# Hybrid attention and pooling layer on one Trainium2 core: key and weight buffers allocated in another order, and four re-orderings in the attention stage

## The chip, the cores and the metric

The kernel runs on 1 core of one Trainium2 chip. The core has a matrix engine (TensorE, PE in the profile, with its weight loads shown as PEld), a vector engine (VectorE, DVE), an activation engine (ScalarE, ACT), a general engine (GpSimd, POOL) and a queue engine that here only issues transfers (SyncE, SP). The metric is the device time of one execution in microseconds (us); the time before is 1195.26 us, the median of 3 runs (1193.7 to 1197.1).

## The reference

One layer on 4096 tokens of width 1024, in float32. The input is normalised and projected once; the projection splits into queries (8 heads of 64), keys and values (2 heads), an attention gate, a pooling input and a pooling gate. Attention is banded: a block of 128 queries sees the block before, its own and the one behind. The pooling half takes centred means over 2, 4, 8 and 16 tokens. Both halves are gated, projected back, normalised and added to the input:

```python
h = rmsnorm(x, pre_norm_g[l])
proj = jnp.einsum('bsd,de->bse', h, w_in[l])
q, k, v, g_a, u_p, g_p = jnp.split(proj, splits, axis=-1)
a = banded_attention(q, k, v, rel_bias, attn_sink[l]) * jax.nn.silu(g_a)
p = multiscale_pool(u_p, pool_w[l], pool_scale[l]) * jax.nn.silu(g_p)
mixed = jnp.einsum('bse,ed->bsd', jnp.concatenate([a, p], axis=-1), w_out[l])
x = x + rmsnorm(mixed, post_norm_g[l])
```

In banded_attention a softmax over up to 384 keys is taken with a relative bias and a sink logit per head.

## The kernel before

Every float32 operand is carried as a pair of float16 tensors (a high part and a rest), and a product is three float16 matmuls. A first stage (to about 500 us) normalises x, stores its pairs to a scratch in DRAM (x_scr) and makes the gates and the pooling half, which go to ga_scr and yp_scr. The last thing that it stores is the gate tile cc (transfers ga_scr<-cc, line L671).

The second stage handles the tokens backwards, in units of 256 tokens (unit 15 first) that hold two blocks of 128 (block 31 first). Its steps, with the names that the profile uses:

- proj_k, proj_v (matmuls kv, L1227 and L1373) and keep_k, keep_v: the projected keys and values lie in one PSUM accumulator. ACT writes a high part (L1216) and DVE the rest (L1217), keys into k_all, values into vv. A unit's keys and values leave in the order ACT keys, DVE keys, ACT values, DVE values.
- proj_q (aq, L1227), in two halves of four heads, and keep_q: ACT and DVE copy it to q.
- visit(b, half): scores (s, L1272) for four heads into two PSUM tiles s0 and s1, then softmax: logits (DVE, p<-s, L1295), exps (ACT, p<-p, L1306), denominators (DVE, L1313 and L1316), probs (ACT, the high part of pn, L1328), rests (DVE, the low part of pn, L1336) and turn (SP, a transposing transfer pt<-pn, L1345). Each of logits, exps, probs and rests is four instructions, one for each head.
- attend(b): values (o, L1417) reads pt and vv; gate (DVE, at, L1425); in an even block then sums (DVE, L1485, L1488, L1491). ACT and POOL split the results into pairs (y and ys, L1452 and L1456).
- the output projection of a unit, in seven products ("11", "22", "12", "s2", "s3", "s1", "s4") of twelve matmuls each (m and ms, L1550) against prepared weight tiles wo. Products go to PSUM accumulators acc0, acc1 and acc2. Product "12" adds onto "11" in acc0; then square (ACT, jkb<-m, L1573) and gain11 (DVE, mo<-m, L1578) both read acc0, the second of the two waiting for the first. The next matmuls into acc0 are the next unit's first half of aq.

The order of the second stage is written by hand. A list (plan) takes entries due(t, function); t is a planned time, not a measured one, and the whole list is sorted by t and emitted in that order. Each engine runs its own instructions strictly in that order. pe(us, ...) puts a TensorE step at the running time now[0] and moves it on. Most units follow one pattern; block 29 (b == NB - 3) is written out apart, because unit 15 is the first to be projected out. There do_kv(u - 1, 1) puts the keys and values of unit 13 into acc1, the accumulator that product "s2" of unit 15 writes next (mix_p6).

Buffers of the second stage come from a pool (pb1) that is laid over memory of the first stage. A tile's first write therefore waits for the first stage's last users of exactly that memory, and the order of allocation decides which users these are.

## Time and profile before

| | |
|---|---|
| median of 3 runs | 1195.26 us (1193.7 to 1197.1) |
| the profiled execution | 1197.77 us |
| its span | 1196.0 us |
| PE busy | 1158.1 us (97%) |
| DVE busy | 933.1 us (78%) |
| ACT busy | 701.2 us (59%) |
| POOL busy | 314.2 us (26%) |
| mean granted clock | 0.996 |

The span is what the trace covers; the time of the execution holds 1.77 us more. A busy time is the sum over an engine's instructions. The granted clock is the share of full speed that TensorE was given. In a row of the timeline the columns are start and duration in us, the engine, line, operation and tiles, how many instructions are merged (x), and in brackets the idle time ahead of it with what ended it. In a row of waits they are the waiting engine, tile and line, the releaser, and the total in us, the number of times and the longest. In a row of windows they are the stretch, its length, busy time of PE, PEld, DVE, ACT and POOL, the granted clock, the DMA share and GB/s.

### The profile page before, as it was taken

The numbers are of one execution on the slowest core, as the hardware profiler recorded it, in microseconds if no ns is written. First come the engines' busy times: TensorE is split into PE (matmuls) and PEld (weight loads), VectorE is DVE, ScalarE is ACT, GpSimd is POOL, SyncE is SP. The second block draws the span as 40 slices with busy tenths as digits, with TensorE's granted clock in tenths as the row PEclk, the third lists the DMA queues.
The fourth block names the chain that finished last, engine by engine and source line by source line (L and its number), as shares of the span: only waits on it lengthen the run. The fifth ranks groups of instructions, "written<-read, shape, count | busy, mean of one in ns | idle before, by whom it ended". The sixth has DMA issues, their size and how long they took to land. (4 is left out here: it accounts for less than half of the span.)

```text
span 1196.0 us, 31699 instructions
## 1 busy us (share of the span) xinstructions
PE 1158.1 (97%) x13176; PEld 890.0 (74%) x13176; DVE 933.1 (78%) x1834; ACT 701.2 (59%) x1459; POOL 314.2 (26%) x309
## 2 busy tenths in 40 slices
PE   5999999999999999898999999999999999999997
PEld 4998888888988888775667676676666767667643
DVE  6889996967888972567877877877787787787786
ACT  6865555645755531266575675666667567566662
POOL 0002111111101110202334433432533443354231
PEclk9999999999999999999999999999999999999999
DMA  9544587578657573487966875776886587587694
GB/s 322 202 124 150 168 287 233 180 232 270 211 176 250 158 205 103 149 219 188 243 174 135 204 191 114 199 197 152 180 203 159 138 203 192 124 189 162 160 236 124
DMA packets 292433, 224.51 MB, mean 188 GB/s; under 512 B 210704, under 2 KB 251920, under 8 KB 287680
## 3 DMA queue, kind: packets, MB, share of 16 engines
q1 hardware_dynamic: 292288, 222.48, 68.3%
q8 instruction: 103, 1.69, 0.6%
q14 instruction: 42, 0.34, 0.1%
HBM read 113.37 MB, written 60.33 MB: 145 GB/s over the span
## 5 line engine op out<-in xcount | busy, mean ns | idle before, releaser
L634 PEld LDWEIGHTS <-wq 128*128 128x128 f16 x4104 | 401.7, 98 | 52.7 <-issue 2.8
L634 PE MATMUL y<-xt,wq 128*128 128x256 f16 x1512 | 204.1, 273 | 0.9 <-ACT cc L742 0.9
L1306 ACT ACTIVATE p<-p,nm 128x385 f32<-128x385 f32 (+1 forms) x256 | 153.0, 599 | 59.6 <-POOL p L1289 38.0
L1227 PE MATMUL aq<-xb,xb 128*128 128x256 f16 x1024 | 174.9, 274 | 4.6 <-DVE mo L1578 4.6
L1336 DVE SCALAR_TENSOR_TENSOR pn<-p,rd,pn 128x384 f16<-128x384 f32 (+1 forms) x256 | 155.6, 654 | 26.1 <-ACT pn L1328 26.1
L1550 PE MATMUL ms<-wo,ys 128*128 128x512 f16 x720 | 162.7, 379 | 1.8 <-ACT pn L1328 1.8
L1295 DVE CUSTOM_DVE_ANT_0 p<-s,nt,nsink 128x384 f32<-128x384 f32 (+1 forms) x256 | 156.0, 666 | 1.5 <-PE s L1272 1.3
L1328 ACT ACTIVATE pn<-p,rd 128x384 f16<-128x384 f32 (+1 forms) x256 | 136.3, 596 | 23.6 <-ACT p L1306 21.7
L1227 PEld LDWEIGHTS <-xb 128*128 128x128 f16 x1280 | 125.8, 98 | 23.6 <-issue 6.7
L1227 PE MATMUL aq<-xb,xt 128*128 128x256 f16 x512 | 140.4, 274 | 0.0
L1550 PEld LDWEIGHTS <-ys 128*128 128x128 f16 x720 | 69.1, 98 | 83.6 <-issue 3.0
L304 POOL TENSOR_TENSOR yt<-yt,sg 128x512 f32<-128x512 f32 (+2 forms) x32 | 48.0, 1500 | 311.4 <-DVE yt L307 283.0
L1550 PE MATMUL m<-wo,y 128*128 128x512 f16 x540 | 119.6, 379 | 1.4 <-POOL y L1456 0.7
L1550 PEld LDWEIGHTS <-y 128*128 128x128 f16 x540 | 51.5, 98 | 64.8 <-issue 3.6
L1584 POOL TENSOR_TENSOR mo<-mo,gpost 128x512 f32<-128x512 f32 x39 | 63.6, 1630 | 85.6 <-ACT jkb L1573 84.5
L1313 DVE TENSOR_SCALAR den<-den 128x4 f32<-128x4 f32 x64 | 17.3, 271 | 76.9 <-ACT p L1306 76.8
L1417 PE MATMUL o<-pt,vv 128*64 128x256 f16 x1128 | 69.0, 274 | 3.9 <-DMA pt<-pn 3.4
L1227 PEld LDWEIGHTS <-xt 128*128 128x128 f16 x640 | 62.9, 98 | 12.9 <-issue 4.3
L634 PE MATMUL plain<-xb,wq 128*128 128x256 f16 x576 | 68.9, 277 | 3.0 <-ACT xb L446 1.8
L634 PE MATMUL y<-xb,wq 128*128 128x256 f16 x504 | 68.8, 273 | 0.0
L634 PE MATMUL v<-xb,wq 128*128 128x256 f16 x504 | 68.6, 273 | 0.2 <-DVE cc L304 0.2
L634 PE MATMUL v<-xt,wq 128*128 128x256 f16 x504 | 68.6, 273 | 0.0
(207 smaller groups left out, 1912.9 us busy)
## 6 DMA issues: line engine op xcount, KB each, us to landing
nt<-in_xT SPq DMA_DIRECT2D x28, 512.0 KB, 5.4
x_scr<-xb SPq DMA_DIRECT2D x14, 1024.0 KB, 7.2
xb<-x_scr SPq DMA_DIRECT2D x14, 1024.0 KB, 7.5
xr<-in_x SPq DMA_DIRECT2D x28, 512.0 KB, 4.4
out<-xr SPq DMA_DIRECT2D x28, 512.0 KB, 3.7
xn<-in_x SPq DMA_DIRECT2D x27, 512.0 KB, 4.5
ga_scr<-cc SPq DMA_DIRECT2D x64, 128.0 KB, 2.1
raw<-in_w_out SPq DMA_DIRECT2D x16, 512.0 KB, 5.3
```

The costliest lines, as they stand in the source:

```text
L304: eng.tensor_tensor(out=out, in0=in0, in1=in1, op=op)
L634: nc.tensor.matmul(b[:, s], wq[:, slot[q, op], wv, s, k, :], x[:, xv, k, :], start=(first and k + s + wv + xv == 0), stop=(last and k == H ...
L1227: nc.tensor.matmul(acc, w[:, j, k, :], x[:, kh, v, kt, :], start=(n == 0), stop=(n == 3 * KT - 1),)
L1295: nc.vector.tensor_tensor_reduce(out=p_t[b, half][:, hh, :nk], in0=s_t[jj][:, gg, :nk], in1=bias[:, h, lo : lo + nk], scale=negc[:, h : h ...
L1306: nc.scalar.activation(p[:, hh, : nk + 1], p[:, hh, : nk + 1], AF.Exp, bias=nm_t[b, half][:, hh : hh + 1], scale=-1.0, accum_out=den_t[b, ...
L1313: nc.vector.tensor_scalar(out=den, in0=den, scalar1=1.0 / P_SCALE, scalar2=None, op0=ALU.mult)
L1328: nc.scalar.activation(prob_view(b, half)[:, 0, i], p_t[b, half][:, i, :nk], AF.Copy, scale=rd_t[b, half][:, i : i + 1],)
L1336: nc.vector.scalar_tensor_tensor(out=pn4[:, 1, i], in0=p_t[b, half][:, i, :nk], scalar=rd_t[b, half][:, i : i + 1], in1=pn4[:, 0, i], op0= ...
L1417: nc.tensor.matmul(o_ps[a, 2 * half : 2 * half + 2], v[:, vi, kt, a], pt[b, half][:, pi, g, :, i, :], start=(n == 0), stop=(n == last),)
L1550: nc.tensor.matmul(z_t[u, tag], y[:, k, yi, :], wo[o][:, wi, k, :], start=(n == 0 and acc is None), stop=(n == 3 * HK - 1), skip_group_che ...
L1584: eng.tensor_tensor(out=mo, in0=mo, in1=gpost[:, cs], op=ALU.mult)
```

## The change

Four edits. First, k_all and gpost are allocated ahead of the weight tiles, and these in another order. Second, the second half of unit 15's queries is projected straight after the first half, and unit 14's keys and values come between the two visits of block 31. Third, in block 29 the visit's second half and then product "12" come ahead of attend(30), which comes ahead of unit 13's keys and values; before, attend(30) came first, then the visit, the keys and values, and product "12". Fourth, gain11 is due 1.2 before the product's end rather than 0.1 behind it, in every unit from 15 to 2.

```diff
--- before.py
+++ after.py
@@ -1193,15 +1193,15 @@
     ps_o = ctx.enter_context(tc.tile_pool(name="ps_o", bufs=1, space=PSUM, reuse_waits="tile"))
 
 
+    RK = 4 * UT
+    k_all = pb1.tile([P, 2, RK], F16, name="k_all")
+    gpost = pb1.tile([P, D], F32, name="gpost")
     wo = {
         o: pb1.tile([P, 2, HK, 512], F16, name=f"wo{o}")
-        for o in (O11, O21, O22, OT1, OT2, OT4, OT3)
+        for o in (OT4, O11, O21, OT2, OT3, OT1, O22)
     }
     wo[O12] = wo[OT4]
-    gpost = pb1.tile([P, D], F32, name="gpost")
-
-    RK = 4 * UT
-    k_all = pb1.tile([P, 2, RK], F16, name="k_all")
+
     q_t, v_t = {}, {}
 
     def x_half(u):
@@ -1670,7 +1670,7 @@
     def mix_p2(u):
         t = pe(M, product, u, "12", O21, 0, True)
         due(t, square, u, 0, 0, 0)
-        due(t + 0.1, gain11, u)
+        due(t - 1.2, gain11, u)
 
     def mix_p6(u):
         due(pe(M, product, u, "s2", OT2, 1), add, u, (0, HI), (0, HI), 1)
@@ -1714,7 +1714,7 @@
 
     due(now[0] + 1.0, lambda: nc.scalar.activation(dummy, mhalf, AF.Exp))
     do_q(u, 0)
-    now[0] += 1.0
+    do_q(u, 1, 0.9)
     for b in reversed(range(2, NB)):
         u = b // 2
         t0 = now[0]
@@ -1724,22 +1724,20 @@
             due(t0 + 9.0, load_xr, u + 1, 0)
         visit(b, 0)
         if b == NB - 1:
-            do_q(u, 1, 2.8)
             due(now[0] + 0.1, load_x, u - 2)
-            now[0] += 2.5
+            do_kv(u - 1, 2, 2.5)
             visit(b, 1)
-            do_kv(u - 1, 2, 2.5)
-            now[0] += 3.0
+            now[0] += 1.0
         elif b == NB - 3:
             due(free[1], load_wo, OT3)
             mix_p4(u + 1)
             mix_p1(u + 1)
+            visit(b, 1)
+            mix_p2(u + 1)
             attend(b + 1)
-            visit(b, 1)
             due(free[1], load_wo, OT1)
             due(free[1] + 8.0, load_wo, O22)
             do_kv(u - 1, 1)
-            mix_p2(u + 1)
             mix_p6(u + 1)
         elif b % 2:
             mix_p3(u + 2)
```

Three places show what the sorted list makes of it. The semaphore names in brackets say on which engine, or on which hardware DMA queue (DMAHW), an instruction waits.

ACT at the start of the second stage (k_all, vv and q hold keys, values and queries; L1715 is a one-element exponential that brings the table of the function in). Before:

```order
L666 ACTIVATE cc1_123<-cc1_123,cg_76 128x512 [waits DVE_49]
L1216 ACTIVATE k_all_5959<-kv15_5967 128x256 [waits DMAHW4_49,DMAHW5_49,DMAHW3_49,DMAHW6_49,PE_49,Activation_49]
L1216 ACTIVATE vv15_6096<-kv15_5967 128x256 [waits DVE_49]
L1715 ACT_TABLE_LOAD
L1715 ACTIVATE dummy_5960<-mhalf_72 128x1
L1216 ACTIVATE q15_0_6100<-aq15_0_6047 128x512 [waits PE_49]
L1306 ACTIVATE p31_0_6203,den31_0_6201<-p31_0_6203,nm31_0_6200 128x257 [waits DVE_49,Pool_49]
```

With the change:

```order
L666 ACTIVATE cc1_123<-cc1_123,cg_76 128x512 [waits DVE_49]
L1216 ACTIVATE k_all_5951<-kv15_5967 128x256 [waits PE_49]
L1216 ACTIVATE vv15_6096<-kv15_5967 128x256 [waits DVE_49]
L1715 ACT_TABLE_LOAD [waits DMAHW6_49,DMAHW5_49]
L1715 ACTIVATE dummy_5960<-mhalf_72 128x1 [waits Activation_49]
L1216 ACTIVATE q15_0_6100<-aq15_0_6047 128x512 [waits PE_49]
L1216 ACTIVATE q15_1_6152<-aq15_1_6103 128x512 [waits PE_49]
L1306 ACTIVATE p31_0_6231,den31_0_6229<-p31_0_6231,nm31_0_6228 128x257 [waits DVE_49,Pool_49]
```

The first write of k_all no longer waits for four DMA queues; the table load, whose instruction writes a tile that is now on other memory, waits for two of them. The copy of the second half of the queries (q15_1) stands directly behind the first.

TensorE in block 29, the first matmul of each step and the rows with waits (m22 and m11 are products, m11 with wo2 and y12 is product "12"; o30 is the values of block 30; kv13 the keys and values of unit 13; ms2 is product "s2"). Before:

```order
L1550 MATMUL m11_15_6746<-wo0_5951,y11_15_6717 128x512
...
L1417 LDWEIGHTS vv14_6381 [waits DMAHW2_49]
L1417 MATMUL o30_6768<-pt30_0_6605,vv14_6381 64x256 [waits DVE_49]
...
L1272 MATMUL s0_5946<-k_all_5959,q14_1_6653 32x288 [waits DVE_49]
L1272 MATMUL s1_5947<-k_all_5959,q14_1_6653 32x288 [waits DVE_49]
L1227 MATMUL kv13_6868<-xb1_68,xb0_66 128x256 [waits DMAHW6_49]
L1373 MATMUL kv13_6868<-xb0_66,xb1_68 128x128
...
L1550 MATMUL m11_15_6746<-wo2_5952,y12_15_6656 128x512 [waits Activation_49]
L1550 LDWEIGHTS ys2_15_6904 [waits DVE_49,Activation_49]
L1550 MATMUL ms2_15_6993<-wo5_5955,ys2_15_6904 128x512 [waits PE_49]
```

With the change:

```order
L1550 MATMUL m11_15_6734<-wo0_5954,y11_15_6709 128x512
...
L1272 MATMUL s0_5946<-k_all_5951,q14_1_6652 32x288 [waits DVE_49]
L1272 MATMUL s1_5947<-k_all_5951,q14_1_6652 32x288 [waits DVE_49]
L1550 MATMUL m11_15_6734<-wo2_5955,y12_15_6605 128x512 [waits Activation_49]
...
L1417 LDWEIGHTS vv14_6359 [waits DMAHW3_49]
L1417 MATMUL o30_6841<-pt30_0_6613,vv14_6359 64x256 [waits PE_49]
...
L1227 MATMUL kv13_6892<-xb1_68,xb0_66 128x256 [waits DMAHW6_49]
L1373 MATMUL kv13_6892<-xb0_66,xb1_68 128x128
L1550 LDWEIGHTS ys2_15_6925 [waits DMAHW2_49,DVE_49,Activation_49]
L1550 MATMUL ms2_15_6987<-wo5_5956,ys2_15_6925 128x512 [waits PE_49]
```

Product "12" stood between kv13 and ms2 and now stands ahead of o30; ms2 follows kv13 directly, and its first weight load still waits for DVE and ACT.

DVE and ACT around gain11 in a unit of the regular pattern (unit 11). Before, DVE and then ACT:

```order
L1316 RECIPROCAL rd21_1_9998<-den21_1_9997 128x4 [waits DVE_49]
L1336 SCALAR_TENSOR_TENSOR pn21_1_10031<-p21_1_9999,rd21_1_9998,pn21_1_10031 128x384 [waits DMAHW2_49,Activation_49]
L1336 SCALAR_TENSOR_TENSOR pn21_1_10031<-p21_1_9999,rd21_1_9998,pn21_1_10031 128x384 [waits Activation_49] x3
L1578 TENSOR_TENSOR mo11_0_10002<-m11_11_9983,gpost_5958 128x512 [waits Activation_49]
L1589 TENSOR_TENSOR mo11_0_10002<-ms2_11_10055,mo11_0_10002 128x512 [waits PE_49]
L1295 ISA p20_0_10183,nm20_0_10180<-s0_5946,nt_69,nsink_87,negc_86 128x384 [waits PE_49]
```

```order
L1328 ACTIVATE pn21_1_10031<-p21_1_9999,rd21_1_9998 128x384 [waits Activation_49]
L1328 ACTIVATE pn21_1_10031<-p21_1_9999,rd21_1_9998 128x384
L1328 ACTIVATE pn21_1_10031<-p21_1_9999,rd21_1_9998 128x384 [waits Activation_49]
L1573 ACTIVATE jkb11_00_10053,ss11_10004<-m11_11_9983 128x512 [waits PE_49]
L1452 CAST ys3_11_10073<-at22_9929 128x4x128
```

With the change:

```order
L1316 RECIPROCAL rd21_1_9998<-den21_1_9997 128x4 [waits DVE_49]
L1336 SCALAR_TENSOR_TENSOR pn21_1_10031<-p21_1_9999,rd21_1_9998,pn21_1_10031 128x384 [waits DMAHW2_49,Activation_49]
L1336 SCALAR_TENSOR_TENSOR pn21_1_10031<-p21_1_9999,rd21_1_9998,pn21_1_10031 128x384 [waits Activation_49] x2
L1578 TENSOR_TENSOR mo11_0_10002<-m11_11_9983,gpost_5952 128x512 [waits PE_49]
L1336 SCALAR_TENSOR_TENSOR pn21_1_10031<-p21_1_9999,rd21_1_9998,pn21_1_10031 128x384 [waits Activation_49]
L1589 TENSOR_TENSOR mo11_0_10002<-ms2_11_10056,mo11_0_10002 128x512 [waits PE_49]
L1295 ISA p20_0_10183,nm20_0_10180<-s0_5946,nt_69,nsink_87,negc_86 128x384 [waits PE_49]
```

```order
L1328 ACTIVATE pn21_1_10031<-p21_1_9999,rd21_1_9998 128x384 [waits Activation_49]
L1328 ACTIVATE pn21_1_10031<-p21_1_9999,rd21_1_9998 128x384
L1328 ACTIVATE pn21_1_10031<-p21_1_9999,rd21_1_9998 128x384 [waits Activation_49]
L1573 ACTIVATE jkb11_00_10054,ss11_10004<-m11_11_9983 128x512 [waits DVE_49]
L1452 CAST ys3_11_10073<-at22_9929 128x4x128 [waits PE_49]
```

gain11 (L1578) moves from behind the four rests to ahead of the last of them, and waits for TensorE rather than ACT; the square (L1573) now waits for DVE where it waited for TensorE. The matmuls of the next unit's aq, which reuse acc0, wait for DVE before and for ACT now.

## The prediction

> **What bounds the kernel now.** I read the page's engine rows first, then the waits of TensorE, then its timeline from 486 us on, where the change begins.

> ```profile
> span 1196.0 us, 31699 instructions
> PE 1158.1 (97%) x13176; PEld 890.0 (74%) x13176; DVE 933.1 (78%) x1834; ACT 701.2 (59%) x1459; POOL 314.2 (26%) x309
> ```

> TensorE is busy for 97% of the span. No edit adds or removes a matmul, so a time can only come from when TensorE stands still and at what clock it works. The waits of TensorE that the edits touch:

> ```profile
> PE aq L1227 <- DVE mo L1578: 4.6, 13, 0.5
> PE s L1272 <- ACT q L1216: 4.0, 2, 3.3
> PE o L1417 <- DMA pt<-pn: 3.4, 3, 1.9
> PE ms L1550 <- ACT pn L1328: 1.8, 1, 1.8
> ```

> The first row is the regular pattern: thirteen units, each with a stop in front of aq. The others are single stops, most at the start of the second stage. So the argument has two places, the start (500 to 562 us) and the thirteen units.

> **The start, first part: keys, and the two halves of Q.** ACT, SP and PE in the timeline, and the landing time of the gate store:

> ```profile
> 499.98 0.94 SPq L671 DMA_DIRECT2D ga_scr<-cc  x2
> ga_scr<-cc SPq DMA_DIRECT2D x64, 128.0 KB, 2.1
> 502.52 0.38 ACT L1216 ACTIVATE k_all<-kv 128x256 f16<-128x256 f32 x1 [5.22 <-PE aq L1227]
> 503.80 1.28 ACT L1715 ACT_TABLE_LOAD   x1
> 505.20 0.58 ACT L1216 ACTIVATE q<-aq 128x512 f16<-128x512 f32 x1
> 505.83 0.41 PE L1272 MATMUL s<-k_all,q 64*32 64x256 f16 x8 [3.34 <-ACT q L1216]
> ```

> The keys' copy begins at 502.52. The row names PE, but the order of the instructions shows four DMA queues in its wait, and the last gate store, issued up to 500.92, lands 2.1 us later, near 503: the copy waits for the store. Keys, values, table load and the copy of Q follow in one line on ACT, and TensorE, done with aq at 502.49, stands until 505.83. With the change the keys' copy is free of the store; the table load waits for it instead (about 502.5), and the first Q is copied by about 504.5. TensorE does not wait for that, since it goes from the first half of Q straight into the second.

> The stop also costs clock:

> ```profile
> 505.00:507.00 2.00, 0.86 (x32) 0.48 (x40) 0.69 (x1) 0.77 (x3) 0.00 (x0) 0.50 1.00 418
> 511.00:513.00 2.00, 2.00 (x17) 1.68 (x16) 1.68 (x4) 1.20 (x4) 0.15 (x1) 0.84 0.97 410
> 507.76:515.05 7.29, 7.29 (x56) 0.73 1.01 415
> 524.32:529.73 5.41, 5.41 (x64) 1.00 0.47 78
> 548.78:554.25 5.47, 5.47 (x81) 1.00 0.54 101
> ```

> These are windows; the last three (PE alone) are a half of Q at low clock, a half of Q at full clock, and one unit's keys and values. Half clock holds to about 511.6 (0.84 in the last mixed slice) and costs 1.9 us in this half of Q (7.29 for 5.41) and some 0.6 in the scores ahead of it, 2.5 us in all.

> Now the new order, with next starts about 0.1 us ahead of the modelled ends: second half of Q from 502.4 (5.35), scores (0.75 for 256 keys), keys and values of unit 14 (5.3), scores (0.75): 514.6. Then scores of block 30 need s0 and s1 back, and DVE reads them behind the copies of unit 14's keys and values: I allow 2.1 us of waiting (it is 0 if DVE were idle, 3 if every copy comes in between). With scores of 1.1 us the next half of Q starts at 517.8. In the rows above it starts at 524.32: 6.5 us earlier.

> **The start, second part: block 29.** PE, DVE and ACT:

> ```profile
> 542.29 0.39 PE L1550 MATMUL m<-wo,y 128*128 128x512 f16 x1 [0.70 <-POOL y L1456]
> 549.19 0.75 DVE L1425 SCALAR_TENSOR_TENSOR at<-o,gaf,gb 128x512 f32<-128x512 f32 x1
> 551.90 0.69 DVE L1491 TENSOR_TENSOR at<-s,at 128x512 f32<-128x512 f32 x1
> 552.51 0.67 DVE L1295 CUSTOM_DVE_ANT_0 p<-s,nt,nsink 128x384 f32<-128x384 f32 x1
> 554.09 2.75 PE L1550 MATMUL m<-wo,y 128*128 128x512 f16 x12
> 555.82 0.17 DVE L1313 TENSOR_SCALAR den<-den 128x4 f32<-128x4 f32 x1 [0.84 <-ACT p L1306]
> 556.29 0.62 ACT L1328 ACTIVATE pn<-p,rd 128x384 f16<-128x384 f32 x1 [0.50 <-ACT p L1306]
> 556.81 0.36 ACT L1216 ACTIVATE k_all<-kv 128x256 f16<-128x256 f32 x1
> 557.66 0.38 ACT L1216 ACTIVATE vv<-kv 128x256 f16<-128x256 f32 x1
> 558.08 0.42 DVE L1217 SCALAR_TENSOR_TENSOR vv<-kv,vv 128x256 f16<-128x256 f32 x1
> 558.65 0.38 PE L1550 MATMUL ms<-wo,ys 128*128 128x512 f16 x1 [1.81 <-ACT pn L1328]
> ```

> Unit 13's keys and values end at 554.25, product "12" covers 2.75 us behind them, and then "s2" waits 1.81 us. The row says ACT; "s2" writes acc1, which the keys and values must leave first, and their last copy (DVE, 558.08 + 0.42) ends 0.15 us ahead of it. So from keys to "s2" there are 4.4 us, and product "12" hides most of it. The change takes this cover away: "12" has been done earlier, and "s2" comes right behind the keys.

> When does DVE finish that copy then? From 524.32 to the start of "11" at 542.29 plus 2.33 of work (it ends at 544.6) the old order takes 20.3 us. The new one starts at 517.8; I add 1.1 us, because scores and "11" wait a little longer for DVE and POOL, and get 539.2. TensorE then does scores (with 0.5 of waiting), "12", the values of block 30 and the keys and values: 1.6 + 2.7 + 2.1 + 5.3, done at 550.9. On the other engines, from 539.2: ACT's copy of "11" (0.6), four exps (2.5), denominators and the step to the rests (1.1), four rests and gain11 (2.9): logits of the visit's second half start at 546.3. In the old order den comes 3.3 us behind the first logit (552.51, 555.82) and probs 0.5 later. In the new order the gate (0.75) and three sums (0.7 each, the last is the row at 551.90) stand between the four logits: 2.85 more, probs at 552.9. ACT copies the keys behind three probs rather than one (1.6), then DVE keys 0.4, ACT one prob and values 0.5, DVE one rest and values 0.9: 556.2. So "s2" starts at about 556.3, 2.35 us earlier than at 558.65, and not 5.9 us earlier as TensorE alone would allow. TensorE stands for 5.3 us.

> A stop of 3.34 us brought half clock; one of 5.3 us should too. Its price has no row of its own: from below 0 (no drop), from above 3.4 us (half speed lasted from 504.9 to 511.6). I take the 2.5 us of the earlier drop, since that is the same thing. The start in sum: -2.35 + 2.5 = about 0.1 us.

> [...]

> The allocation of wo and gpost I cost at 0: their transfers follow the gate store in SP's queue as before, and the first product that reads them starts 18 us or more behind their landing. Unit 13's x is loaded once Q is done, at 507.8 instead of 515.08, and is needed at 545.

> **The thirteen units.** One unit as an example (all thirteen show the same distances to 0.02 us), then values in four units and the landing of two transposes (us, last column):

> ```profile
> 772.68 2.21 DVE L1336 SCALAR_TENSOR_TENSOR pn<-p,rd,pn 128x384 f16<-128x384 f32 x4 [0.73 <-ACT pn L1328]
> 774.07 0.57 ACT L1573 ACTIVATE jkb<-m 128x512 bf16<-128x512 f32 x1
> 774.55 0.19 ACT L1573 ACTIVATION_READ_ACCUMULATOR jkb<-m 128x1 f32 x1
> 774.81 0.69 DVE L1578 TENSOR_TENSOR mo<-m,gpost 128x512 f32<-128x512 f32 x1
> 774.96 3.64 SPq L1345 DMA_TRANSPOSE pt<-pn  x1
> 775.55 0.27 PE L1227 MATMUL aq<-xb,xb 128*128 128x256 f16 x1 [0.44 <-DVE mo L1578]
> 695.40 2.46 PE L1417 MATMUL o<-pt,vv 128*64 128x256 f16 x36
> 780.88 2.48 PE L1417 MATMUL o<-pt,vv 128*64 128x256 f16 x36
> 823.62 2.16 PE L1417 MATMUL o<-pt,vv 128*64 128x256 f16 x36
> 993.83 2.50 PE L1417 MATMUL o<-pt,vv 128*64 128x256 f16 x36
> pt<-pn SPq DMA_TRANSPOSE x1, 7.2
> pt<-pn SPq DMA_TRANSPOSE x1, 6.0
> ```

> The square runs first, gain11 ends at 775.50, aq starts 0.05 later. With the change gain11 takes the place of the fourth rest, one slot of 0.53 earlier (four rests and the start of gain11: 772.68 to 774.81): 774.28 to 774.97. The square, which now waits for it, takes 0.67 (774.07 to 774.74): 775.01 to 775.68. aq waits for the square now and starts at 775.72, 0.15 to 0.2 later than before. The wait is not removed; the two readers change places and the longer tail is now last. Thirteen times 0.15: +2.0 us. Bounds: 0 (released as the square's main part ends, 0.1 earlier, and the step from ACT is quicker) and 0.2 each, 2.6.

> The fourth rest ends 0.6 later, so its transpose is issued at 775.57 rather than 774.96, while TensorE is 0.15 later: 0.45 us less room. The values behind aq read that transpose in their second half. In four units (starts 695.40, 738.13, 780.88, 993.83) the values take 0.3 us longer than the 2.16 of the other nine: there the transpose lands too late (7.2 us behind its issue), in the others it lands earlier (6.0). Four times 0.45: +1.8 us. Bounds: 0 (the landings come earlier) and 13 times 0.45, 5.9. I take the row's four.

> The sum: 0.1 + 2.0 + 1.8 = 3.9 us, a span of 1199.9 us. The profiled execution was 1197.77 us for a span of 1196.0, 2.5 us above the median of the runs; on the median I forecast 1195.3 + 3.9 = 1199.2 us.

> **Rivals.**

> First, the start keeps its gain (not slower). The place is the 5.3 us stop ahead of "s2"; its price is 2.5 us of clock and 1 us for each us of waiting. If the clock does not drop, the sum is 1.4 us (1196.7); if the copies are also done 2.3 us sooner, so that the stop is 3 us, it is -0.9 (1194.4). It decides at a stop near 3 us. For it: a stop of 1.81 us ahead of 558.65 left the clock full, and my chain has ten terms. Against it: three sums now stand in that chain.

> Second, gain11 does what its place suggests, and the stops in front of aq go (4.6 us in the waits): 1195.3 + 0.1 - 4.6 + 1.8 = 1192.6. It needs a square that is done before gain11; the order has it behind, and ACT as aq's releaser, so I give it little.

> Third, the runs of before mostly have no drop at 505. The stop there is at the edge: the four executions known lie 4.1 us apart (1193.7 to 1197.77), more than the 2.5 us of one drop, and the profiled one, with the drop, is the longest. Then the median carries none, the new stop adds its own, and the change costs 2.5 us more: 1201.7. [...]

> **How the numbers follow.** The forecast 0.45, first rival 0.25, second 0.1, third 0.2. A measurement of this kernel can tell about 0.3%, 3.6 us, from no change. The forecast lies close to that line (slower 0.24, same 0.21); the first rival is mostly same (faster 0.06, same 0.17, slower 0.02); the second faster 0.06, same 0.04; the third slower 0.17, same 0.03. Faster 0.12, same 0.45, slower 0.43. The range goes from 1193.0, which leaves out the second rival and the best of the first, to 1203.0, which takes in the third; the likeliest case's own is 1196.5 to 1201.5.

> **What would show it.** After: PE runs without a stop from 497 to about 514.5 at full clock; k_all is written near 497.3; the waits show "ms" with 4 to 6 us and the granted clock about 0.5 behind it; the row "aq <- DVE mo" is gone and an "aq <- ACT jkb" of about 6.5 us in thirteen times stands in its place; values of more than 2.16 us in at least four units. I am wrong if the wait of "ms" stays under 3 us, or if aq's waits in the units shrink.

## The result

The changed kernel took 1205.92 us (median of five executions, 1205.72 to 1207.16); five executions of the kernel before beside it took 1196.89 us (1193.7 to 1197.1). The ratio is 1.0084, 95% interval 1.0073 to 1.0096: slower by about 9 us. The forecast was 1199.2 us, and its range ended at 1203.

The span of the changed kernel's page, and the waits of TensorE (columns: engine and line that waited, who released it, us in total, times, longest):

```profile
span 1205.0 us, 31670 instructions
...
PE aq L1227 <- ACT jkb L1573: 7.1, 13, 0.7
...
PE ms L1550 <- ACT vv L1216: 4.9, 1, 4.9
...
PE ms L1550 <- DVE mo L1589: 2.7, 6, 0.5
PE o L1417 <- DMA pt<-pn: 2.3, 5, 0.6
...
PE m L1550 <- DVE mo L1589: 1.3, 1, 1.3
```

The first (about 6.5 us in the forecast, with ScalarE as releaser), the second (4 to 6) and that of o were forecast. The third, product "s4" behind an add of VectorE, was not: the kernel before had no such wait. The last is a single product near the end, which waited 0.7 us in the kernel before.

Both profiled executions in stretches, worked out from the starts of aq (the first half of unit 15's Q, the first half of unit 13's Q, and the same thirteen units later):

| stretch | before | after | difference |
|---|---|---|---|
| up to the first aq (first stage, the same program) | 497.09 | 497.86 | +0.77 |
| start: first aq to aq of unit 13 | 65.10 | 66.38 | +1.28 |
| thirteen units | 554.42 | 561.48 | +7.06 |
| from there to the end | 79.39 | 79.28 | -0.11 |
| span | 1196.0 | 1205.0 | +9.0 |

The thirteen units' ends are these four rows of the two timelines (before, then after):

```profile
562.19 0.28 PE L1227 MATMUL aq<-xb,xb 128*128 128x256 f16 x1
...
1116.61 0.27 PE L1227 MATMUL aq<-xb,xb 128*128 128x256 f16 x1 [0.44 <-DVE mo L1578]
```

```profile
564.24 0.28 PE L1227 MATMUL aq<-xb,xb 128*128 128x256 f16 x1
...
1125.72 0.27 PE L1227 MATMUL aq<-xb,xb 128*128 128x256 f16 x1 [0.62 <-ACT jkb L1573]
```

So most of the loss, 7.06 of 9.0 us, is in the units. A unit of the changed kernel, in the order of time, on five engines' rows (aq of this unit starts at 866.28; ys and y are the float16 pairs of the results, the streams of the output projection, and nsink holds the sink logits, one for each head):

```profile
864.82 0.68 DVE L1578 TENSOR_TENSOR mo<-m,gpost 128x512 f32<-128x512 f32 x1
...
865.54 0.60 ACT L1573 ACTIVATE jkb<-m 128x512 bf16<-128x512 f32 x1 [0.83 <-DVE mo L1578]
...
869.05 1.15 POOL L1456 TENSOR_TENSOR ys<-yf,ys 128x512 f16<-128x512 f32 x1
870.15 0.31 POOL L1289 COPY p<-nsink 128x4 f32<-128x4 f32 x2
...
870.37 0.62 ACT L1306 ACTIVATE p<-p,nm 128x385 f32<-128x385 f32 x1 [2.60 <-POOL p L1289]
...
885.73 0.68 DVE L1589 TENSOR_TENSOR mo<-ms,mo 128x512 f32<-128x512 f32 x1
...
886.47 1.89 PE L1550 MATMUL ms<-wo,ys 128*128 128x512 f16 x8 [0.46 <-DVE mo L1589]
```

And the same steps in the kernel before (aq at 861.20):

```profile
859.73 0.58 ACT L1573 ACTIVATE jkb<-m 128x512 bf16<-128x512 f32 x1
...
864.32 0.32 POOL L1289 COPY p<-nsink 128x4 f32<-128x4 f32 x2
864.55 0.62 ACT L1306 ACTIVATE p<-p,nm 128x385 f32<-128x385 f32 x1 [2.60 <-POOL p L1289]
...
880.11 0.69 DVE L1589 TENSOR_TENSOR mo<-ms,mo 128x512 f32<-128x512 f32 x1
...
880.87 1.47 PE L1550 MATMUL ms<-wo,ys 128*128 128x512 f16 x6
```

Measured from the start of aq, the square (jkb) starts 0.73 us later than before (-0.74 instead of -1.47). Behind it on ScalarE stand the casts of the streams. GpSimd makes their low parts (L1456) and copies the sinks behind these (L1289), and the exps of the next block wait for that copy: they start 0.74 us later (4.09 instead of 3.35). VectorE's add of "s1" ends at 20.13 instead of 19.60, and "s4", which writes the same accumulator, is the one that waits. aq is the first thing the later square holds up, and "s4", 20 us on, the second.

### The profile page after: what moved, and what is told of

Read it like the earlier page. It is cut to its first block, busy times and chain, and to the rows that moved or that the text cites. A ratio compares the mean times of both kernels' runs of the same rounds, so it can differ in the third digit from the quotient of the medians.

```text
span 1205.0 us, 31670 instructions
## 1 busy us (share of the span) xinstructions
PE 1159.6 (96%) x13176; PEld 890.3 (74%) x13176; DVE 932.6 (77%) x1834; ACT 702.8 (58%) x1459; POOL 315.5 (26%) x309
## 5 line engine op out<-in xcount | busy, mean ns | idle before, releaser
L1306 ACT ACTIVATE p<-p,nm 128x385 f32<-128x385 f32 (+1 forms) x256 | 153.0, 599 | 63.1 <-POOL p L1289 33.8
L1227 PE MATMUL aq<-xb,xb 128*128 128x256 f16 x1024 | 174.5, 274 | 7.1 <-ACT jkb L1573 7.1
L1336 DVE SCALAR_TENSOR_TENSOR pn<-p,rd,pn 128x384 f16<-128x384 f32 (+1 forms) x256 | 157.8, 658 | 28.1 <-ACT pn L1328 28.1
L1550 PE MATMUL ms<-wo,ys 128*128 128x512 f16 x720 | 164.9, 383 | 7.8 <-ACT vv L1216 4.9
L1295 DVE CUSTOM_DVE_ANT_0 p<-s,nt,nsink 128x384 f32<-128x384 f32 (+1 forms) x256 | 156.1, 665 | 0.1
L1328 ACT ACTIVATE pn<-p,rd 128x384 f16<-128x384 f32 (+1 forms) x256 | 136.3, 596 | 24.1 <-ACT p L1306 21.0
L1227 PEld LDWEIGHTS <-xb 128*128 128x128 f16 x1280 | 125.7, 98 | 23.1 <-issue 6.3
L1227 PE MATMUL aq<-xb,xt 128*128 128x256 f16 x512 | 140.4, 274 | 0.0
L1550 PEld LDWEIGHTS <-ys 128*128 128x128 f16 x720 | 70.2, 98 | 90.8 <-issue 8.4
L1550 PE MATMUL m<-wo,y 128*128 128x512 f16 x540 | 119.7, 379 | 1.6 <-DVE mo L1589 1.3
L1550 PEld LDWEIGHTS <-y 128*128 128x128 f16 x540 | 51.5, 98 | 65.2 <-issue 4.7
L1313 DVE TENSOR_SCALAR den<-den 128x4 f32<-128x4 f32 x64 | 17.8, 278 | 85.9 <-ACT p L1306 85.6
L1227 PEld LDWEIGHTS <-xt 128*128 128x128 f16 x640 | 62.9, 98 | 15.3 <-issue 6.8
L1417 PE MATMUL o<-pt,vv 128*64 128x256 f16 x1128 | 68.9, 274 | 2.4 <-DMA pt<-pn 2.3
## 6 DMA issues: line engine op xcount, KB each, us to landing
ga_scr<-cc SPq DMA_DIRECT2D x64, 128.0 KB, 2.1
```

The source lines that it names most:

```text
L1227: nc.tensor.matmul(acc, w[:, j, k, :], x[:, kh, v, kt, :], start=(n == 0), stop=(n == 3 * KT - 1),)
L1295: nc.vector.tensor_tensor_reduce(out=p_t[b, half][:, hh, :nk], in0=s_t[jj][:, gg, :nk], in1=bias[:, h, lo : lo + nk], scale=negc[:, h : h ...
L1306: nc.scalar.activation(p[:, hh, : nk + 1], p[:, hh, : nk + 1], AF.Exp, bias=nm_t[b, half][:, hh : hh + 1], scale=-1.0, accum_out=den_t[b, ...
L1313: nc.vector.tensor_scalar(out=den, in0=den, scalar1=1.0 / P_SCALE, scalar2=None, op0=ALU.mult)
L1328: nc.scalar.activation(prob_view(b, half)[:, 0, i], p_t[b, half][:, i, :nk], AF.Copy, scale=rd_t[b, half][:, i : i + 1],)
L1336: nc.vector.scalar_tensor_tensor(out=pn4[:, 1, i], in0=p_t[b, half][:, i, :nk], scalar=rd_t[b, half][:, i : i + 1], in1=pn4[:, 0, i], op0= ...
```

## The experiments

Each run is compared with executions of the kernel before on the same chip (medians 1195.3 to 1195.9 us there; the row of the change is the result above, against 1196.89 us). "Start" and "units" are the stretches of the table above, from the profiled execution alone; the median holds for all executions. The two stretches left out vary as well: the first aq starts at 497.1 to 498.0 us, and behind the units come 77.0 to 79.4 us. So the units are the sharpest measure, and a difference of 2 us between medians need not lie in the stretch that an edit touches.

| run | against the kernel before | median us | ratio, 95% interval | start | units |
|---|---|---|---|---|---|
| e6_keys | keys' allocation | 1192.58 | 0.998, 0.9971 to 0.9989 | 60.11 | 554.52 |
| e3_keys_q | and the change's second edit (Q side by side) | 1195.62 | 1.0001, 0.9992 to 1.0011 | 63.03 | 555.74 |
| e1_gain_late | and the products' order | 1195.84 | 1.0005, 0.9996 to 1.0015 | 64.37 | 554.45 |
| (the change) | and gain11 early | 1205.92 | 1.0084, 1.0073 to 1.0096 | 66.38 | 561.48 |
| e2_gain_early | gain11 early alone | 1204.14 | 1.0071, 1.0053 to 1.0088 | 64.24 | 561.48 |
| e8_sink | sinks' copy earlier | 1197.84 | 1.0015, 1.0006 to 1.0025 | 64.79 | 556.16 |
| e7_early_sink | e2 and e8 together | 1200.83 | 1.0044, 1.0029 to 1.0059 | 62.15 | 560.89 |
| e5_gain_gap2 | gain11 in VectorE's gap | 1194.18 | 0.999, 0.9981 to 1.0 | 62.35 | 551.51 |
| e10_cover | e1, "12" behind the keys | 1193.64 | 0.9986, 0.9977 to 0.9995 | 60.39 | 555.23 |
| e11_cover_gap | e10 and e5 | 1193.17 | 0.9981, 0.9973 to 0.999 | 62.86 | 551.78 |
| e12_keys_gap | e6 and e5 | 1191.79 | 0.997, 0.996 to 0.9981 | 62.00 | 551.53 |

Two runs are not in it: e4_gain_gap, which did not do what it was for, and e9_fill_gap, whose order of the start differs.

### Which part is it: gain11

e1_gain_late is the changed kernel with one line put back:

```diff
-        due(t - 1.2, gain11, u)
+        due(t + 0.1, gain11, u)
```

> The changed kernel with gain11 put back behind the square (due t + 0.1), all else of the change kept. Theory U (the loss lies in the units, 12 periods of 43.2 instead of 42.65 us, and comes from gain11 standing ahead of the square: aq's stop 0.19 longer each, and the later square pushes the stream casts, the sink copy, the exps and at last the product 's4' back): the waits 'ms <- DVE mo' (2.7 us) and 'aq <- ACT jkb' (7.1) go, 'aq <- DVE mo' is back at 4.6, and the time is 6.9 us below the changed kernel: 1199.0 us, 2.1 above before. Rival A (the units lose because of the other allocation or the moved products, which change what is fetched when): the units stay at 43.2, the time within 1 us of the changed kernel, 1205 to 1206.

e2_gain_early is the kernel before with the same line changed the other way.

> The kernel before with gain11 alone moved ahead of the square (due t - 1.2). Theory U: all thirteen units show the rows of the changed kernel ('aq <- ACT jkb' 7.1, 'ms <- DVE mo' 2.7 more), 1196.9 + 6.9 = 1203.8 us, and the start stays as before (a stop of 3.3 us ahead of the scores at 505). Rival A: 1197 to 1199 us, since the aq stops alone are worth 2.5 (7.1 - 4.6).

The waits of TensorE between 565 and 1120 us in e1_gain_late and in the changed kernel; in the kernel before there is only the row of aq with its 4.6 us. The stretch holds the units, but for the last stop ahead of aq (at 1125.72) in the changed kernel.

```profile
PE aq L1227 <- DVE mo L1578: 4.6, 13, 0.5
PE o L1417 <- DMA pt<-pn: 0.4, 2, 0.3
```

```profile
PE aq L1227 <- ACT jkb L1573: 6.4, 12, 0.7
PE ms L1550 <- DVE mo L1589: 2.7, 6, 0.5
PE o L1417 <- DMA pt<-pn: 2.0, 4, 0.6
```

In e2_gain_early the same three rows stand, with 6.4, 2.8 and 2.0 us.

Theory U holds. With gain11 late the units take 554.45 us, as before; with gain11 early, and nothing else of the change, 561.48, to the hundredth what the whole change takes. Allocation and product order have no part in it, and rival A falls. The times go further than the units did: e2 is 8.8 us slower than before, not 6.9, and e1 0.5 slower, not 2.1. By the profiles, the 1.8 us that e2 loses beyond its units lie outside them, where start and end vary; no run here traces them further.

### Through which chain: the copy of the sinks

e7_early_sink adds to e2 that GpSimd's copy of the sinks is issued 3 us earlier, ahead of the streams' casts (the copy and its tiles come out of the function of the first logit into one of their own); e8_sink does that alone.

```diff
     def softmax(b, half, t):
+        due(t - 3.0, sink, b, half)
```

> The kernel before with gain11 moved as in the change (the run e2_gain_early, 1204.1 us) and in addition the copy of the sinks, which GpSimd makes ahead of the first exp of each half visit, issued 3 us earlier, so that it goes ahead of the casts of the streams on GpSimd. Theory U (the second half of the units' loss is the chain square, stream casts on ACT, GpSimd's lows, sink copy, exps, rests, adds, product 's4'): the row 'ms <- DVE mo' (2.8 us) goes, 'aq <- ACT jkb' stays at 7.0, and the period falls from 43.19 to about 42.8 us: 1204.1 - 12 x 0.4 = 1199.3 us. Rival D (the add of 's1' is late for VectorE's own order alone): 'ms <- DVE mo' and the period stay, 1203 to 1205.

> The control for e7_early_sink: the same earlier copy of the sinks in the kernel before, gain11 in its old place. Theory U: exps are earlier here too, but TensorE has no wait on that chain, only the 4.6 us ahead of aq, which hang on the probs and the square: 1194 to 1196 us.

TensorE's waits in the units of e7_early_sink (without the last stop ahead of aq), then over its whole span:

```profile
PE aq L1227 <- ACT jkb L1577: 8.7, 12, 1.0
PE o L1421 <- DMA pt<-pn: 2.2, 4, 0.7
...
PE aq L1227 <- ACT jkb L1577: 9.5, 13, 1.0
```

"ms <- DVE mo" is gone, as theory U had it, and rival D falls: measured from aq, the add ends at 19.60 again, though the square is as late as in e2 (-0.74). Yet the units are only 0.6 us shorter than in e2, since aq waits 9.5 us rather than 7.0. Most of that is a price of the earlier copy itself, which the control shows: its aq waits 6.4 us rather than 4.6, and its units take 1.74 us more than before, where I expected no difference. GpSimd and VectorE in one unit of e8_sink, then VectorE in the kernel before:

```profile
850.15 1.18 POOL L1287 COPY p<-nsink 128x4 f32<-128x4 f32 x1
851.29 1.15 POOL L1460 TENSOR_TENSOR y<-yf,y 128x512 f16<-128x512 f32 x1
851.97 1.01 DVE L1489 TENSOR_TENSOR s<-at,yf 128x512 f32<-128x512 f32 x1
```

```profile
850.67 0.87 DVE L1485 TENSOR_TENSOR s<-at,yf 128x512 f32<-128x512 f32 x1
```

In one of a unit's four half visits the earlier copy stands ahead of a low part (y<-yf). VectorE's first sum (s<-at,yf) runs beside that low part and ends 0.54 us behind it in both kernels (852.98 and 852.44 in e8; 851.54 and 851.00 before). In e7 and e8 it takes 1.01 or 1.02 us in all thirteen units, where it takes 0.87 in the kernel before and in e2. VectorE's work from there to gain11 is later by as much: 13 times 0.14 is 1.8 us, what aq's stops grow by. That the sum waits for the low part is argued from these rows.

Taken against this control, the units give the size of the chain. Early gain11 costs them 7.06 us without the early copy and 560.89 - 556.16 = 4.73 with it: 2.3 us go through the chain. Unit by unit it is clearer. In the six units whose "s4" waits in e2, early gain11 costs 0.69 to 0.72 us; with the early copy it costs 0.19 or 0.20 in five of them and 0.46 in one. Near the end comes one product more, whose wait grows from 0.7 to 1.3 us without the early copy and stays at 0.4 with it: 0.6 us. So the chain is shown, and its size is about 3 us. The medians say 8.8 - 3.0 = 5.8 us (1.0044 and 1.0015 are 5.0 and 2.0 us), with an uncertainty of some 3 us, and they hold the varying start and end too.

### Where gain11 costs nothing

e4_gain_gap moved gain11 to t - 3.3, into VectorE's idle time between the reciprocal and the first rest.

> The kernel before with gain11 alone moved still earlier (due t - 3.3), into VectorE's idle time of 0.73 us between the reciprocal and the four rests, so that the last rest and the square end as before. Theory U: the square ends at 774.74 on the old unit's scale and aq is released there, in time, so the stops ahead of aq (4.6 us) go, while the rests and their transposes end as before: 1196.9 - 4.6 = 1192.3, or up to 1.4 more (1193.7) where transposes are late for an earlier aq. Rival C (gain11 waits for the copy of 'm' there and holds the rests up by its own 0.7 us): transposes later, o and s stops grow, 1197 to 1203.

It took 1252.96 us (ratio 1.0487, 1.0464 to 1.051) and tells nothing on the theories (its stops show something on the clock, below): at t - 3.3 gain11 was issued ahead of product "12", so it multiplied product "11", which stands in acc0 then, and "12" had to wait for it, as the page of this run shows (a group of instructions: busy, mean, idle before and its releaser).

```profile
L1550 PE MATMUL m<-wo,y 128*128 128x512 f16 x540 | 139.6, 419 | 48.7 <-DVE mo L1578 47.6
```

e5_gain_gap2 mends that by issuing the product earlier too, with its place on TensorE unchanged:

```diff
-        t = pe(M, product, u, "12", O21, 0, True)
+        due(now[0] - 0.8, product, u, "12", O21, 0, True)
+        now[0] += M
+        t = now[0]
         due(t, square, u, 0, 0, 0)
-        due(t + 0.1, gain11, u)
+        due(t - 3.3, gain11, u)
```

> What the run e4_gain_gap meant to do: in the kernel before, product '12' is issued 0.8 us earlier in the program (its place on TensorE is the same), so that gain11 can stand between the reciprocal and the four rests and still read its own product. Theory U: gain11 ends near 772.6 on the old unit's scale, the square as before at 774.74, so acc0 is free before TensorE has done its scores (775.11): the stops ahead of aq (4.6 us) go, rests and transposes end as before. 1195.3 - 4.6 = 1190.7 us, up to 1.4 more where transposes are late for an earlier aq. Rival C (gain11 holds the rests up): stops of o and ms grow, 1197 to 1203.

Its waits in the units:

```profile
PE o L1417 <- DMA pt<-pn: 2.1, 5, 0.6
PE ms L1550 <- DVE mo L1589: 0.6, 3, 0.2
```

The stops ahead of aq are gone, all 4.6 us, since both readers of acc0 are done before TensorE comes back to it. In their place late transposes (o) show 2.1 us and "s4" 0.6. A part of the 2.1 is not new: the four late values of the kernel before, 0.3 us each, made no row. The units are 2.9 us shorter; the median is only 1.7 us lower, at the edge of what can be told. What is shown is where gain11 has to stand: in time that VectorE would idle, ahead of the rests, not among them.

### The start, part by part

e6_keys changes the allocation alone.

```diff
+    RK = 4 * UT
+    k_all = pb1.tile([P, 2, RK], F16, name="k_all")
+    gpost = pb1.tile([P, D], F32, name="gpost")
-        for o in (O11, O21, O22, OT1, OT2, OT4, OT3)
+        for o in (OT4, O11, O21, OT2, OT3, OT1, O22)
```

> The kernel before with the allocation of keys and wo alone changed; both halves of Q, products and gain11 as before. By the prediction's step the copy of the keys no longer waits for the gate store: k_all is written near 498 instead of 502.5, the table load waits for it instead, the first Q is copied by about 504.5, and the stop ahead of the scores (3.3 us in the profile of before) shrinks by about 1.3 us to 2.0: 1194.0 to 1195 us. Rival: the copy of Q waits for the same store or table, the stop stays at 3.3: no difference, 1195 to 1196.

e3_keys_q adds the change's second edit, the two halves of Q side by side and unit 14's keys and values between the two visits of block 31.

```diff
     do_q(u, 0)
-    now[0] += 1.0
+    do_q(u, 1, 0.9)
...
         if b == NB - 1:
-            do_q(u, 1, 2.8)
             due(now[0] + 0.1, load_x, u - 2)
-            now[0] += 2.5
+            do_kv(u - 1, 2, 2.5)
             visit(b, 1)
-            do_kv(u - 1, 2, 2.5)
-            now[0] += 3.0
+            now[0] += 1.0
```

> The kernel before with the allocation of keys and wo and both halves of Q side by side; the output products stay behind the values, gain11 stays behind the square. If the two clock drops of the changed kernel (after 517 and after the 4.9 us stop of 's2') eat the start's gain, and the second belongs to product '12' having left its place, then here '12' stands behind unit 13's keys again, the 4.9 us stop shrinks to about 2 and no drop follows it: the start is 3 to 5 us earlier than before, 1192 to 1194 us. Rival B (the exps and copies of block 30 are late after Q side by side in any case, and the gain is given back at the next wait): 1196 to 1198.

The timeline of e6_keys, ScalarE and then TensorE:

```profile
497.88 0.38 ACT L1216 ACTIVATE k_all<-kv 128x256 f16<-128x256 f32 x1
...
499.16 1.28 ACT L1715 ACT_TABLE_LOAD   x1
...
503.12 0.60 ACT L1216 ACTIVATE q<-aq 128x512 f16<-128x512 f32 x1 [2.47 <-PE aq L1227]
505.63 0.51 ACT L1306 ACTIVATE p<-p,nm 128x257 f32<-128x257 f32 x1 [1.91 <-DVE nm L1295]
...
503.77 0.30 PE L1272 MATMUL s<-k_all,q 64*32 64x256 f16 x8 [0.69 <-ACT q L1216]
...
542.42 1.17 PE L1417 MATMUL o<-pt,vv 128*64 128x256 f16 x18 [1.09 <-DMA pt<-pn]
```

The same first exp, and the values of block 30, in e3_keys_q:

```profile
510.55 0.51 ACT L1306 ACTIVATE p<-p,nm 128x257 f32<-128x257 f32 x1 [1.28 <-DVE nm L1295]
...
544.85 1.49 PE L1417 MATMUL o<-pt,vv 128*64 128x256 f16 x12 [4.13 <-DMA pt<-pn]
```

The allocation alone is worth 2.8 us, twice what I expected. Neither the table load (499.16) nor the copy of Q (503.12) waits for the gate store. Of the 3.34 us stop ahead of the scores 0.69 are left, and the clock stays at 1.00 behind it. The second edit, Q side by side, then gives it all back. TensorE runs unbroken there, but the first exp starts at 510.55 rather than 505.63, and values of block 30, which need the last of the transposes behind those exps, stand for 4.13 us instead of 1.09. The granted clock fell to 0.50 in that stop and stayed there for 6.8 us (it was 1.00 in e6_keys). As I read it, what paces this stretch is the softmax on VectorE and ScalarE, and the first scores are what starts it; no run separates the halves of Q from the new place of unit 14's keys. Rival B is right in that the gain is given back, though it named other waits.

e10_cover is e1 with "12" back behind unit 13's keys and values in block 29 (and the values of block 30 still behind block 29's scores).

```diff
             visit(b, 1)
-            mix_p2(u + 1)
             attend(b + 1)
...
             do_kv(u - 1, 1)
+            mix_p2(u + 1)
             mix_p6(u + 1)
```

> The changed kernel with gain11 back in its old place and, in block 29, product '12' put back behind unit 13's keys and values, where it covers their copies; the values of block 30 stay behind the scores of block 29. By the prediction's reading (the 4.9 us stop ahead of 's2' is there because '12' no longer covers the copies) that stop goes; instead the values of block 30 stand where '12' stood and wait about 2.6 us for the last transpose (it lands near 544.6 in the runs so far). 's2' starts near 555.2 instead of 556.9: 1.7 us below the run e1_gain_late, 1194 us. Rival: the copies still wait for exps on ScalarE, and 's2' starts at 556.9 or later whatever stands ahead of it: 1195.5 to 1197.

Its values of block 30 and its product "s2":

```profile
544.47 1.17 PE L1417 MATMUL o<-pt,vv 128*64 128x256 f16 x18 [1.48 <-DMA pt<-pn]
...
554.51 1.67 PE L1550 MATMUL ms<-wo,ys 128*128 128x512 f16 x7 [0.87 <-ACT vv L1216]
```

1193.64 us, 2.2 below e1 (1.7 expected). The stop ahead of "s2", 4.8 us in e1, shrinks to 0.87, and 1.48 appear at the values. The prediction's reading holds: "12" had been the cover of those copies.

e9_fill_gap tried to fill the same stop with other work: e1 with gain11 as in e5, and unit 13's first half of Q ahead of "s2".

```diff
             do_kv(u - 1, 1)
+            do_q(u - 1, 0, 5.0)
             mix_p6(u + 1)
...
-            do_q(u - 1, 0, 2.0 * (b == NB - 2))
+            if b != NB - 4:
+                do_q(u - 1, 0, 2.0 * (b == NB - 2))
```

> A version of my own: the change's keys, halves of Q and earlier product '12', gain11 in the gap as in e5_gain_gap2, and the first half of unit 13's Q moved from behind block 28's first scores to ahead of product 's2', where TensorE of the changed kernel stands for 4.9 us. Theory U: that stop and its clock drop go (4.9 + about 1.5), and the stops ahead of aq go (4.6): 1195.8 - 4.9 - 1.5 - 4.6 = about 1185 us. Rival: copies and exps are the limit of the start, the stop only moves to the scores or values behind it: 1189 to 1192.

1200.39 us, ratio 1.0035 (1.0021 to 1.0048): slower, and worse than the rival allowed. Q ran where the stop had been, but as I read it block 28 then had too little for TensorE to do while the softmax went on: values of block 29 waited 2.0 us for a transpose, and "s4" 4.0 us for an add of VectorE. The clock fell to 0.50 behind the second stop, and "s4" took 4.44 us for 2.75. Its first matmuls:

```profile
584.86 1.50 PE L1550 MATMUL ms<-wo,ys 128*128 128x512 f16 x4 [3.98 <-DVE mo L1589]
```

Two further runs put together what had been faster alone.

> As e10_cover, with gain11 in VectorE's gap as in the run e5_gain_gap2, which took the 13 units from 554.4 to 551.5 us. The two gains lie in different stretches and should add: 1194.0 - 2.9 = 1191 us, or 1192.3 if only the 1.7 us of e5's medians carry over. Rival: the start's clock drop comes and goes with its stops and hides the sum, 1193 to 1195.

> The two parts that were each faster alone, together: the keys' allocation (e6_keys, -2.8 us) and gain11 in VectorE's gap (e5_gain_gap2, -1.7 us by its medians, -2.9 us over the 13 units). They lie in different stretches, the start and the units, and should add: 1195.4 - 2.8 - 1.7 = 1190.9 us, 1189.7 by the units. Rival: the transposes that are late for an earlier aq (stops of o) take the units' part back, as they did in e11_cover_gap (0.5 us of 2.9 left): 1192 to 1193 us.

e11_cover_gap: 1193.17 us, the rival's value, and for the rival's reason. Its units are 551.78 us, so they keep their gain. Its start is 62.86 us where e10's is 60.39: the clock was 0.57 from 518 to 522 us (1.00 in e10), and the half of Q there took 7.08 us instead of 5.41; "s2" then waited 2.0 us for the copy of the values instead of 0.9.

e12_keys_gap: 1191.79 us, ratio 0.997 (0.996 to 0.9981), between theory and rival, but not for the rival's reason. Its units are 551.53 us, as short as in e5. What is missing lies in the start, 62.00 us where e6 has 60.11: "s2" stood for 2.08 us instead of 1.79, the clock fell to 0.50 behind it, and "s2" took 4.44 us instead of 2.75. It is the fastest version here, 3.5 us ahead of the kernel before and some 14 ahead of the changed one: the allocation from the change, nothing else of it, and gain11 in the gap.

## Why the prediction was wrong

**The sum of the units failed.** The prediction had two terms there, 2.0 us (aq) and 1.8 (transposes), 3.8 in all; the units lost 7.06. Both terms were about right: aq's stops went from 4.6 to 7.1 us, +2.5 (0.19 a unit, forecast 0.15 to 0.2), with ScalarE as the releaser. The transposes were late in exactly four units; the values there took 2.88, 2.89, 2.74 and 2.82 us instead of 2.46 to 2.50, +1.4 together. What was missing is a third term, put at nothing without a reason: what is queued behind the square on ScalarE, which the step "the square, which now waits for it" stopped short of. That leaves 7.06 - 2.5 - 1.4 = 3.2 us in the units, 2.7 of them in one row of the waits ("s4" behind the add), and 0.6 more came at the product near the end (other waits of the end shrank). The rest of the 9.0 us of the two profiles against the 3.9 forecast is 1.2 us of the start (below) and 0.8 us of the first stage, whose program is the same. The kernel before showed the chain among ScalarE's waits:

```profile
ACT p L1306 <- POOL p L1289: 38.0, 15, 2.6
```

TensorE did not wait on it only because the add of "s1" ended 0.07 us ahead of "s4" (880.11 + 0.69, and 880.87). I had costed the delay where it is felt first, and not asked who else waits. None of the signs that I had named for being wrong looks there: aq's waits grew, "ms" waited over 3 us, and the prediction failed all the same.

**The start's sum held, its parts were partly luck.** I had -2.35 us for the earlier "s2" and +2.5 for the clock, +0.1 in all; the three parts of the start measure +0.5 us together (e1, interval -0.5 to +1.8), and the one profile of the change +1.28. In e1_gain_late "s2" starts 59.21 us behind the first aq (556.92, 497.71), 61.56 before (558.65, 497.09): -2.35, as worked out. The stop ahead of it was 4.8 us (4.9 in the changed kernel, forecast 5.3), the granted clock behind it 0.50, and "s2" took 4.37 us there, 4.96 in the changed kernel's own profile, for 2.75: a price of 1.6 to 2.2 us. But the step from the store to the table load was wrong ("the table load waits for it instead"): the order lists two DMA queues for the load, but it waits for nothing (it starts at 499.33 in the changed kernel, ahead of the store), and the keys gave 2.8 us. Nor did I see that the second edit takes 3.0 us, because I costed it by the place of later matmuls and not by the first exp.

**One stop was not seen as dangerous.** I had allowed 2.1 us of waiting ahead of block 30's scores, and it was 1.49 + 0.25 (below). In the profile of the changed kernel the clock fell behind it, and the next half of Q took 7.1 us instead of 5.4: 1.7 us, more than the whole +1.28 by which that profile's start is longer. That execution, at 1207.16 us, was the longest of the five.

**The rivals.** The first needed a stop without a drop, and the stop was punished. The second, gain11 taking aq's stops away, fails for the place the change gives it and holds for another place (e5). The third, that the profile of before carries a drop that most of its other executions lack, is half borne out. Of six profiles with nearly the same program up to there, the clock fell to 0.50 behind the stop ahead of the first scores in three (before, e2 and e8, starts of 65.10, 64.24 and 64.79 us), and stayed at 1.00 in three (e4, e5 and e7, starts of 62.91, 62.35 and 62.15). So the drop comes and goes; how often it does in the kernel before is not known, nor how much of it is in the median. Its 1201.7 us lie below the 1205.92 measured, because it too had the units at 3.8 us.

## What to carry to other kernels

When an instruction is delayed, follow its own engine's queue and not only its output: here 0.7 us on a square cost about 3 us through the casts, a small copy and the exps behind it, and 2.5 us at the matmul that waited for the square. A margin of 0.07 us between a release and its waiter shows as no wait at all in a profile, so look at what stands just short of waiting. And at the start of a pipelined stage, look first at what starts the slowest chain: here TensorE without a break bought nothing, since the first exp came 4.9 us later. A stop can also bring half clock behind it: here it followed stops of 3.34 us (the kernel before) and 2.08 us (e12) and one of 1.49 and 0.25 us (the changed kernel), it cost about 1.7 us in the one that lasted 3.41 us, and behind the same 1.49 and 0.25 us in e1 it did not come.

## What the hardware showed

**The same stop was followed by half clock in one profile and not in another.** Scores of block 30 in the changed kernel, then windows of TensorE (us, busy with the number of matmuls, granted clock, DMA share, GB/s):

```profile
516.96 0.68 PE L1272 MATMUL s<-k_all,q 64*32 64x384 f16 x24 [1.49 <-DVE nm L1295]
517.88 0.68 PE L1272 MATMUL s<-k_all,q 64*32 64x384 f16 x24 [0.25 <-DVE nm L1295]
...
515.00:518.00 3.00, 1.26 (x72) 1.00 1.06 425
518.00:520.00 2.00, 2.00 (x32) 0.65 1.42 215
```

And e1_gain_late, the same instructions with the same waits:

```profile
515.00:518.00 3.00, 1.26 (x64) 1.00 1.06 428
518.00:520.00 2.00, 2.00 (x39) 1.00 1.51 180
```

Both were busy for 1.26 of 3.0 us; one was at 0.50 behind it (from 520 to 522) and the other at 1.00. Six profiles have this stop, 1.49 and 0.25 us, and the clock fell behind it in two (the changed kernel and e11). So neither the length of the stop nor the busy share tells these two apart.

**Half clock came in pieces of 3.41 us here.** Windows of TensorE (the same columns) in the kernel before, then in the changed kernel; the stretches at full clock are 3.41 us long too, counted from a drop of the same trace:

```profile
501.40:504.82 3.42, 1.09 (x11) 1.00 0.88 285
504.82:511.64 6.82, 5.50 (x67) 0.50 1.01 424
556.02:559.43 3.41, 1.60 (x8) 1.00 0.83 343
559.43:562.84 3.41, 3.41 (x64) 1.00 0.49 92
1160.18:1163.59 3.41, 1.67 (x60) 1.00 0.79 180
1163.59:1167.00 3.41, 3.28 (x29) 1.00 0.00 0
```

```profile
515.20:518.62 3.42, 1.68 (x74) 1.00 1.04 420
518.62:522.03 3.41, 3.41 (x18) 0.50 1.22 178
522.03:525.44 3.41, 3.41 (x32) 1.00 0.95 226
552.75:556.16 3.41, 0.81 (x15) 1.00 1.03 313
556.16:562.98 6.82, 4.49 (x11) 0.50 0.50 102
562.98:566.40 3.42, 3.42 (x70) 1.00 1.02 297
```

In these windows half clock lasted 6.82 us in the kernel before, and 3.41 and 6.82 us in the changed one. In the stretch ahead of these drops TensorE idled for 2.33, 1.74 and 2.60 us. In the kernel before 1.81 us of idling (from 556.02) and 1.74 us (from 1160.18) brought none. Why a drop followed the 1.74 us at the scores of block 30, and not the 1.74 us there, stays open.

```profile
740.46:743.87 3.41, 1.13 (x6) 1.00 0.00 0
743.87:747.28 3.41, 3.41 (x10) 0.50 0.31 58
788.25:791.66 3.41, 1.63 (x8) 1.00 0.00 0
791.66:795.07 3.41, 3.41 (x18) 1.00 0.49 90
```

The first stop put 3.41 - 1.13 = 2.28 us of idling into one stretch, and the clock fell. The second was cut into 1.72 and 1.78 us by the edge of a stretch, and it did not. All this is read from single profiles; no run moved a stop against these stretches on purpose.

**A copy of 128x4 elements on GpSimd** took 0.19 us in one place and 1.18 in another (858.59 in e7_early_sink, 850.15 in e8_sink). In all thirteen units of e8 the long one ended 0.04 to 0.06 us behind an instruction of VectorE (L1615: 849.79 + 1.49 us, against 850.15 + 1.18), and so did the copy of 0.65 us in the units of the kernel before (behind L1485: 850.67 + 0.87, against 850.94 + 0.65). That GpSimd waited for VectorE there is argued; spans on GpSimd are rough, and no run tests it.
